# Feed-forward stages of a hybrid decoder step: 512-column weight parts, a seeded PSUM bank and a TensorE order written out

## The chip, the cores and the metric

The kernel runs on one core of one Trainium2 chip. The metric is the device time of one execution in microseconds (us); "before" is the median of three runs. All traces are of one profiled execution.

## The reference, cut to what matters

One step of a decoder layer over 1032 tokens (1024 of a prompt, 8 single decode tokens): a half-step feed-forward network, a mixer (dilated attention and a state space scan), cross attention, a second half-step feed-forward network, and a final norm. The change touches the two feed-forward networks alone:

```python
def swiglu(x, w_gate, w_up, w_down):
    return (jax.nn.silu(x @ w_gate) * (x @ w_up)) @ w_down
...
    x = x + (0.5 * swiglu(rms_norm(x, g_ffn1), w1_gate, w1_up, w1_down)).astype(x.dtype)
    ...
    x = x + (0.5 * swiglu(rms_norm(x, g_ffn2), w2_gate, w2_up, w2_down)).astype(x.dtype)
```

with x of 1032 x 1024, the two wide weights 1024 x 2816 and the third 2816 x 1024, all float32.

## The kernel before, in words

**Precision.** Each float32 factor is split in two float32r parts, hi (a rounding copy) and lo (the rest). A product takes three matmuls: hi hi, hi lo, lo hi (`three`, L341 to L345).

**Products of 2 x 2 blocks.** Tokens, which run along the columns of every matmul, fall in three groups: P0 and P1 of 388 columns, and R of 256. P0 and P1 go through a seven-product form of the 2 x 2 block product (Winograd's form of Strassen's algorithm): the weight side needs A11, A12, A21, A22 and the sums S1 = A21 + A22, S2 = S1 - A11, S3 = A11 - A21, S4 = A12 - S2; the token side B11, B21, B22 and T1 to T4. Then C11 = A11 B11 + A12 B21, C12 = U2 + S1 T1 + S4 B22, C21 = U3 + A22 T4, C22 = U3 + S1 T1, with U2 = A11 B11 + S2 T2 and U3 = U2 + S3 T3. Group R is multiplied plainly with the A blocks, in matmuls of 256 columns.

**Loops.** `ffn` walks over pairs of 128 hidden features. `gate_up(m)` runs twice per pair (22 per network): it makes gate and up products of 128 hidden features; its two weight loads of 512 KB give A11, A12 (gate) and A21, A22 (up). `down(m0)` then multiplies the pair's hidden values with two rows of blocks of the third weight and adds to x: two halves c of the output, two units u each (10 per network). The last pair is done plainly by `down_last`. A `gate_up` has 84 matmuls of 388 columns and 48 of 256, and a `down` has as many. In `gate_up` each weight block has four chunks j of 128 columns, each with its own input.

**Weights.** `weights` (L307) makes each factor in pieces of 256 columns: DVE forms a sum where one is needed (L321), ACT casts to hi (L331), DVE and POOL in turn subtract to get lo (L332). Parts live in a ring of four tiles of 1024 columns (tag "w"): one is the sums of the block, three hold two pieces with hi and lo each. Raw weights have two tiles (tag "wr"), loaded on the SP queue (L338).

**PSUM.** A `gate_up`, or a unit of `down`, has a set of four banks: b1, b2, b3 for the seven products and rb for group R; sets are taken from the pools anew and in turn. `ORDER` (L355) lists the products with bank, token factor and whether the bank starts anew. `evac` follows each: A11's product is copied to SBUF as `e["s"]` by ACT (L389, L469), and added wherever U2 or U3 is needed (by DVE in `gate_up`, L392, L398, L418; by POOL in `down`, L472, L478, L485). S1's and S4's results are read from b3 by DVE (L401, L404); S4's product is added to b3 after S1's result has been read. In `down` DVE adds each bank to x (L471 to L486).

**Who sets the order.** The program is traced, and a planner with a timing model orders each engine's instructions; TensorE's too, so products of one block and of the next, R's and the seven, lie mixed on TensorE. Each engine then runs its queue in that order, and waits on semaphores.

Of the kernel before, what the change touches and what calls it, by code (L numbers as in the profile page):

```python
# [10 lines left out]
F32 = mybir.dt.float32  # L11
# [9 lines left out]
T = SEQ + NDEC  # L21
# [31 lines left out]
def _shape_constants():  # L53
    """Arrays that depend on the shapes alone."""
# [11 lines left out]
    # decode tokens' heads on the partitions: token b's head e in row 32 (b % 4) + 8 (b // 4) + e, and in row 8 b + e  # L66
# [10 lines left out]
def tile_step(ctx, tc, a, o):  # L77
# [59 lines left out]
    def banks(shape, bufs):  # L137
        """Divides the last two banks anew."""
# [27 lines left out]
    def rstd(out, ms):  # L166
        """out = 1/sqrt(ms + eps) for a few columns: an estimate from the exponent, then Newton's steps."""
# [10 lines left out]
    def rstd_row(acc, one):  # L178
        """1/rms of up to 400 tokens on all partitions (in PSUM), from sums of squares by feature."""
# [21 lines left out]
    def nstat(N, x, k, ti, eng=nc.gpsimd):  # L201
        """Adds the squares of a finished block; after the last one the row 1/rms."""
# [10 lines left out]
    def nsplit(N, x, k, s):  # L213
        """hi/lo parts of x * gain."""
# [7 lines left out]
    def wload(src, dve=0, dst=None):  # L222
        """Loads a block of weights and splits it in two float32r parts, w = hi + lo."""
# [26 lines left out]

# [16 lines left out]
    def factors(es, side, F, names):  # L267
        """Tiles for the parts of a normalized input, block by block of its features."""
# [38 lines left out]
    def weights(raw):  # L307
        """Hi/lo parts of a weight block's factors, 256 columns at a time."""
        S = {}
        sums = wt("fs", F32)  # L310
        done = []

        def get(name, c):
            if name in raw:
                return raw[name][:, c * 256:(c + 1) * 256]
            if (name, c) not in S:
                p, q, op, i = {"S1": ("A21", "A22", OP.add, 0), "S2": ("S1", "A11", OP.subtract, 1),
                               "S3": ("A11", "A21", OP.subtract, 0), "S4": ("A12", "S2", OP.subtract, 1)}[name]
                p, q = get(p, c), get(q, c)
# [4 lines left out]
        def mat(name, c):  # L324
            src = get(name, c)
            i = len(done) % 2 * 512
            if not i:
                st["wt"] = wt("fw", F32R)
# [1418 lines left out]
```

## Time and profile before

| what | value |
|---|---|
| runs, us | 2729.35, 2729.98, 2732.21; median 2729.98 |
| profiled execution, span from first to last instruction, us | 2729.3 |
| granted TensorE clock, mean | 0.973 of full speed |
| first network's products, us of the span | about 106 to 841 |
| second network's products, us of the span | about 1948 to 2709 |

The profiled execution's span lies 0.7 us under the median, so times of the trace can be set against the runs as they are. The profile page gives busy shares by engine and in 40 slices of the span; matmuls are pipelined, so their busy share says little, and the start-to-start distance of matmuls in the timeline is what is read for TensorE's rate. A wait is shown in the timeline in brackets, with what ended it.

### The profile page before, as it was taken

What the parts mean: (1) busy time and instruction counts of PE and PEld (TensorE: products, weight loads), DVE (VectorE), ACT (ScalarE), POOL (GpSimd) and SP (SyncE); (2) the same over time, 40 slices, a digit from 0 to 9 for tenths busy, and PEclk for the clock granted to TensorE, in tenths of its full rate; (3) what the DMA queues carried; (4) which work ended last, traced back from release to release, by engine and by line L of the source; (5) the groups of instructions that cost most, each with busy time, mean ns of one, the idle gap of its engine ahead of it and who ended that gap; (6) DMA issues with size and microseconds to landing.
All of it is one profiled execution on the core that took longest, in us unless ns stands there. A gap on an engine that the chain in (4) does not pass through costs nothing. (4 is left out here: it accounts for less than half of the span.)

```text
span 2729.3 us, 44428 instructions
## 1 busy us (share of the span) xinstructions
PE 2512.2 (92%) x15995; PEld 2380.5 (87%) x15995; DVE 2118.6 (78%) x4455; ACT 1179.2 (43%) x2817; POOL 1314.5 (48%) x1246
## 2 busy tenths in 40 slices
PE   6999999999999999987987899989799999999998
PEld 5899999999998999886676799978689999999997
DVE  7677787888876668989789957564888888787886
ACT  5533333344344456554466423233443333333345
POOL 5555555555563114436365644102455555555553
PEclk8999999999999999998998999999899999999999
DMA  5411112111123222235755324573011111111112
GB/s 168 133 48 60 59 57 62 56 56 56 56 67 111 63 62 83 80 117 188 232 181 173 110 72 137 174 234 98 17 47 47 47 47 47 54 49 53 49 47 78
DMA packets 274404, 243.81 MB, mean 89 GB/s; under 512 B 17008, under 2 KB 246056, under 8 KB 274176
## 3 DMA queue, kind: packets, MB, share of 16 engines
q1 hardware_dynamic: 272512, 240.88, 28.7%
q8 instruction: 126, 2.06, 0.3%
q14 instruction: 94, 0.77, 0.1%
q10 hardware_dynamic: 1672, 0.09, 0.0%
HBM read 200.02 MB, written 45.75 MB: 90 GB/s over the span
## 5 line engine op out<-in xcount | busy, mean ns | idle before, releaser
L331 ACT CAST fw<-fs 128x256 fp32r<-128x256 f32 x512 | 192.7, 405 | 446.3 <-DVE fs L321 303.7
L332 POOL TENSOR_TENSOR fw<-fs,fw 128x256 fp32r<-128x256 f32 x256 | 216.4, 846 | 343.4 <-ACT fw L331 329.1
L235 POOL TENSOR_TENSOR wl<-wr,wh 128x1024 fp32r<-128x1024 f32 (+4 forms) x79 | 168.3, 2131 | 406.4 <-ACT wh L231 393.6
L332 POOL TENSOR_TENSOR fw<-fraw,fw 128x256 fp32r<-128x256 f32 x262 | 212.0, 815 | 108.6 <-ACT fw L331 95.4
L331 ACT CAST fw<-fraw 128x256 fp32r<-128x256 f32 x524 | 187.9, 403 | 158.0 <-PE pd L345 53.3
L332 DVE TENSOR_TENSOR fw<-fs,fw 128x256 fp32r<-128x256 f32 x256 | 159.3, 622 | 60.7 <-ACT fw L331 60.6
L321 DVE TENSOR_TENSOR fs<-fraw 128x256 f32<-128x256 f32 x256 | 166.7, 667 | 29.7 <-DMA fraw<-in_w_up_dram 26.1
L332 DVE TENSOR_TENSOR fw<-fraw,fw 128x256 fp32r<-128x256 f32 x262 | 141.6, 541 | 59.4 <-ACT fw L331 57.8
L345 PE MATMUL pd<-hRh,fw 128*128 128x256 f32 x640 | 136.6, 280 | 0.0
L231 ACT CAST wh<-wr 128x1024 fp32r<-128x1024 f32 (+1 forms) x80 | 76.6, 958 | 99.6 <-PE pwa L245 41.4
L472 POOL TENSOR_TENSOR x<-x,ts 128x388 f32<-128x388 f32 x80 | 93.3, 1175 | 45.0 <-PE pd L345 37.9
L345 PEld LDWEIGHTS pd<-hRh,fw 128*128 128x128 f32 x640 | 110.5, 189 | 0.0
L478 POOL TENSOR_TENSOR x<-x,ts 128x388 f32<-128x388 f32 x80 | 91.2, 1161 | 36.6 <-DVE x L477 36.6
L418 DVE TENSOR_TENSOR tu<-pg,ts 128x388 f32<-128x388 f32 x44 | 24.7, 562 | 107.3 <-PE pg L345 107.3
L856 DVE SCALAR_TENSOR_TENSOR tg<-xr,hv,tg 128x344 f32<-128x344 f32 (+1 forms) x108 | 84.2, 786 | 16.8 <-ACT tg L854 16.1
L485 POOL TENSOR_TENSOR x<-x,ts 128x388 f32<-128x388 f32 x80 | 89.1, 1113 | 15.8 <-DVE x L484 15.8
L245 PE MATMUL pxbc<-xh,wh 128*128 128x344 f32 x288 | 96.6, 335 | 0.0
L245 PE MATMUL pxbc<-xl,wh 128*128 128x344 f32 x288 | 95.7, 332 | 0.0
L245 PE MATMUL pxbc<-xh,wl 128*128 128x344 f32 x288 | 95.4, 331 | 0.0
L321 DVE TENSOR_TENSOR fs<-fraw,fs 128x256 f32<-128x256 f32 x128 | 93.7, 732 | 1.9 <-POOL fw L332 1.8
L245 PE MATMUL pqkv<-xh,wh 128*128 128x344 f32 x288 | 93.7, 325 | 0.5 <-ACT tg L207 0.5
L245 PE MATMUL pqkv<-xh,wl 128*128 128x344 f32 x288 | 93.2, 324 | 0.0
(801 smaller groups left out, 9773.9 us busy)
## 6 DMA issues: line engine op xcount, KB each, us to landing
fraw<-in_w_gate_dram SPq DMA_DIRECT2D x44, 512.0 KB
fraw<-in_w_up_dram SPq DMA_DIRECT2D x44, 512.0 KB
fraw<-in_w_down_dram SPq DMA_DIRECT2D x44, 512.0 KB
wr<-in_w_in_dram SPq DMA_DIRECT2D x32, 512.0 KB
x_scr<-x SPq DMA_DIRECT2D x16, 516.0 KB
x<-x_scr SPq DMA_DIRECT2D x16, 516.0 KB
bc<-acs_scr SPq DMA_DIRECT2D x16, 512.0 KB
ckv<-in_cache_mem_k_dram SPq DMA_DIRECT2D x16, 512.0 KB
```

What stands on the lines that cost most here:

```text
L231: nc.scalar.copy(hi[:, :w], raw[:, :w])
L235: e.tensor_sub(lo[:, q], raw[:, q], hi[:, q].bitcast(F32))
L245: nc.tensor.matmul(ps, w, v, start=i == 0, stop=i == last)
L321: nc.vector.tensor_tensor(t, p, q, op=op)
L331: nc.scalar.copy(hi, src)
L332: (nc.vector if len(done) % 2 else nc.gpsimd).tensor_sub(lo, src, hi.bitcast(F32))
L345: nc.tensor.matmul(ps, l[:, js], m, start=bool(start and not i), stop=bool(stop and i == 2), skip_group_check=True)
L418: nc.vector.tensor_add(u0, b2, e["s"])
L472: nc.gpsimd.tensor_add(xa[:, P1], xa[:, P1], e["s"])
L478: nc.gpsimd.tensor_add(xb[:, P1], xb[:, P1], e["s"])
L485: nc.gpsimd.tensor_add(xb[:, P0], xb[:, P0], e["s"])
L856: nc.vector.scalar_tensor_tensor(cv, raw[:, i:i + c], hw(i), cv, op0=OP.mult, op1=OP.add)
```

## The change

Only `ffn` and its helpers change (the other hunks drop comments):

- The pieces of weights are 512 columns wide: a whole block with its four chunks in `gate_up`; two blocks of 256 (A11 with A21, S1 with S2, A12 with A22, S3 with S4) in `down`. One ring tile holds hi and lo of one piece. Sums in `gate_up` are 512 wide, in `down` 256.
- The sums have a tile of their own, in the room of the row 1/rms (`held`), for all blocks but the first of a network; the four ring tiles then all hold parts. S3 is written over S1, and S4 over S2.
- A11's product is copied by ACT from b1 into b2 (PSUM to PSUM), and S2's product is added onto that. So U2 and U3 are plain ACT copies of b2 in `gate_up` (DVE adds before), C21 needs one DVE instruction less, and in `down` the three POOL adds of `e["s"]` per unit go. A matmul per set at the start of a network writes b2 once, so that later matmuls add to it.
- The eight banks are taken once per network, as two fixed sets.
- In S4's evac for odd m, T2's two steps come ahead of B22 and T3. In `down` each unit's evac follows its own matmuls.
- `tc.manual_schedule(engines={PE})` around each `gate_up` and each `down`: TensorE runs a block's instructions in the order in which the program emits them. Where they fall among those of other blocks, and the order on the other engines, stay the planner's. The emitted order of `gate_up` is A11, R by A11, S2, A12, R by A12, S3, S1, S4, A22, R by A22, R by A21; in the first block of a network all of R comes last. In `down`, for each c: A11, R by A11, R by A21, S1, S2, A12, R by A12, S3, S4, A22, R by A22.

```diff
-            hi, lo = st["wt"][:, i:i + 256], st["wt"][:, i + 256:i + 512]
-            nc.scalar.copy(hi, src)
-            (nc.vector if len(done) % 2 else nc.gpsimd).tensor_sub(lo, src, hi.bitcast(F32))
+    def two(n):
+
+        t = wt("fw", F32R)
+        return t[:, :n], t[:, n:2 * n]
+
+    def split(hl, src, like=lambda t: t):
+
+        hi, lo = like(hl[0]), like(hl[1])
+        st["turn"] = not st.get("turn")
+        nc.scalar.copy(hi, src)
+        (nc.vector if st["turn"] else nc.gpsimd).tensor_sub(lo, src, hi.bitcast(F32))
+        return hl
...
-    ORDER = (("A11", 0, "B11", True), ("S2", 1, "T2", True), ("A12", 0, "B21", False), ("S3", 1, "T3", False),
+    ORDER = (("A11", 0, "B11", True), ("S2", 1, "T2", False), ("A12", 0, "B21", False), ("S3", 1, "T3", False),
              ("S1", 2, "T1", True), ("S4", 2, "B22", False), ("A22", 1, "T4", False), ("A21", None, None, False))
...
+        def sums_of(m):
+            if not m:
+                return wt("fs", F32)
+            if not held:
+                held.append(rp.tile([128, T], F32, name="fs", tag="r"))
+            return held[0]
+
+        sets = [[PD("fb") for _ in range(3)] + [PO("fb")], [flat(PT("fb")) for _ in range(2)] + [PS("fb"), PS("fb")]]
...
+        for bk, _ in sets:
+            h = F["B11"][0][0]
+            nc.tensor.matmul(bk[1], h[:, :128], h, start=True, stop=True, skip_group_check=True)
...
+            def mat(name):
+                if name == "S2":
+                    add_up("S1", t, sums[:, :512])
+                if name in SUMS and name not in t:
+                    add_up(name, t, sums[:, :512] if name == "S3" else sums[:, 512:1024])
+                return split(two(512), t[name])
...
             def evac(name):
                 if name == "A11":
-                    e["s"] = acc_(PA)
-                    nc.scalar.copy(e["s"], b1)
+                    nc.scalar.copy(b2, b1)
                 elif name == "S2":
                     e["U2"] = acc_(PA)
-                    nc.vector.tensor_add(e["U2"], b2, e["s"])
+                    nc.scalar.copy(e["U2"], b2)
...
                 elif name == "S3":
                     e["U3"] = acc_(PA)
-                    nc.vector.tensor_add(e["U3"], b2, e["s"])
+                    nc.scalar.copy(e["U3"], b2)
                 elif name == "S1":
                     e["u1"] = sq_(PA)
                     nc.vector.tensor_add(e["u1"], b3, e["U3"])
...
                         b12, t1 = Hd["b"]
+                        nc.vector.tensor_sub(t1, u1, t1)
+                        put(Hd["T2"], t1, nc.vector)
                         put(Hd["B22"], u1, nc.gpsimd)
                         nc.vector.tensor_sub(b12, u1, b12)
-                        nc.vector.tensor_sub(t1, u1, t1)
-                        put(Hd["T2"], t1, nc.vector)
                         put(Hd["T3"], b12, nc.gpsimd)
                 elif name == "A22":
                     u0, u1 = sq_(PA), e["u1"]
-                    nc.vector.tensor_add(u0, b2, e["s"])
-                    nc.vector.scalar_tensor_tensor(u0, u0, 0.5, e["g0"], op0=OP.mult, op1=OP.mult)
+                    nc.vector.scalar_tensor_tensor(u0, b2, 0.5, e["g0"], op0=OP.mult, op1=OP.mult)
...
                 if name == "S3":
-                    early = {("S1", c): mat("S1", c) for c in range(2)}
...
+                    early["S1"] = mat("S1")
+                w = early.pop(name, None) or mat(name)
+                if f:
+                    for j in range(4):
+                        three(bk[b], w, j, F[f][j], first and j == 0, j == 3)
+                if f:
+                    evac(name)
+                if name[0] == "A" and not late:
+                    rest(name, w)
...
                     if name == "A11":
-                        e["s"] = acc_(PA)
-                        nc.scalar.copy(e["s"], b1)
+                        nc.scalar.copy(b2, b1)
                     elif name == "S2":
                         add(xa[:, P1], xa[:, P1], b2)
-                        nc.gpsimd.tensor_add(xa[:, P1], xa[:, P1], e["s"])
...
+                    need(name)
+                    w = W[name]
+                    if f:
                         for e in U:
-                            three(e["b"][b], w, e["j"], Hd[t], first, True)
+                            three(e["b"][b], w, e["j"], Hd[f], first, True)
+                            evac(name, e)
...
             for i in range(2):
-                gate_up(m + i)
+                with tc.manual_schedule(engines={mybir.EngineType.PE}):
+                    gate_up(m + i)
...
             if m < last:
-                down(m)
+                with tc.manual_schedule(engines={mybir.EngineType.PE}):
+                    down(m)
```

## Rows read from the trace of the kernel before

**Rows 1.** Profile page: busy us, share of the span and instructions of each engine.

```profile
PE 2512.2 (92%) x15995; PEld 2380.5 (87%) x15995; DVE 2118.6 (78%) x4455; ACT 1179.2 (43%) x2817; POOL 1314.5 (48%) x1246
```

**Rows 2.** Stretches: us, busy PE, PEld, DVE, ACT, POOL (count), granted clock, DMA share, GB/s.

```profile
148.83:810.65 661.82, 632.24 (x3962) 615.59 (x3961) 532.74 (x1046) 258.75 (x692) 374.47 (x402) 1.00 0.19 57
2019.12:2681.34 662.22, 632.97 (x3962) 615.68 (x3960) 536.34 (x1047) 257.00 (x691) 370.59 (x398) 1.00 0.16 49
595.50:613.00 17.50, 17.50 (x115) 17.50 (x114) 10.47 (x23) 6.73 (x18) 6.00 (x9) 1.00 0.17 61
613.00:634.00 21.00, 18.30 (x116) 17.39 (x114) 20.97 (x41) 9.55 (x26) 15.15 (x16) 1.00 0.15 42
```

**Rows 3.** Timeline (start us, us, engine, instruction) of TensorE in a `gate_up`: S1's end, R, A22, S4.

```profile
605.69 0.34 PE L345 MATMUL pg<-T13h,fw 128*128 128x388 f32 x1
605.87 0.28 PE L345 MATMUL pg<-R4h,fw 128*128 128x256 f32 x1
...
607.53 0.34 PE L345 MATMUL pg<-T40h,fw 128*128 128x388 f32 x1
...
609.64 0.34 PE L345 MATMUL pg<-B220h,fw 128*128 128x388 f32 x1
...
611.80 0.28 PE L345 MATMUL pg<-R0h,fw 128*128 128x256 f32 x1
```

**Rows 4.** TensorE's waits in ten pairs of the first network: us, times, longest.

```profile
PE pd L345 <- ACT T2h L264: 18.7, 10, 2.7
PE pd L345 <- DVE fw L332: 8.5, 10, 0.9
```

**Rows 5.** Timeline at a `down`'s first wait: ACT and TensorE.

```profile
618.06 0.51 ACT L264 CAST T2h<-tu 128x388 fp32r<-128x388 f32 x1 [1.31 <-DVE tu L413]
...
618.64 0.42 PE L345 MATMUL pd<-B22h,fw 128*128 128x388 f32 x1 [1.76 <-ACT T2h L264]
```

**Rows 6.** Timeline of DVE about S1's and S4's results in a `gate_up`.

```profile
606.07 0.56 DVE L401 TENSOR_TENSOR tu<-pg,ts 128x388 f32<-128x388 f32 x1 [0.52 <-PE pg L345]
...
609.84 0.56 DVE L418 TENSOR_TENSOR tu<-pg,ts 128x388 f32<-128x388 f32 x1 [2.88 <-PE pg L345]
```

**Rows 7.** Timeline of the second network's first block, TensorE.

```profile
1951.02 0.43 PE L345 MATMUL pg<-B210h,fw 128*128 128x388 f32 x1
...
1964.99 0.69 PE L345 MATMUL pg<-T20h,fw 128*128 128x388 f32 x1 [11.60 <-ACT T20h L264]
...
1980.69 0.53 PE L345 MATMUL pg<-T23h,fw 128*128 128x388 f32 x1
1983.31 0.69 PE L345 MATMUL pg<-T30h,fw 128*128 128x388 f32 x1 [2.10 <-DVE ts L392]
```

**Rows 8.** Groups by line and shape: count, busy us, mean ns, idle before.

```profile
L480 DVE TENSOR_TENSOR x<-x,pd 128x388 f32<-128x388 f32 x80 | 43.7, 546 | 0.0
L321 DVE TENSOR_TENSOR fs<-fraw,fs 128x256 f32<-128x256 f32 x128 | 93.7, 732 | 1.9 <-POOL fw L332 1.8
L321 DVE TENSOR_TENSOR fs<-fs,fraw 128x256 f32<-128x256 f32 x128 | 52.0, 435 | 0.0
L472 POOL TENSOR_TENSOR x<-x,ts 128x388 f32<-128x388 f32 x80 | 93.3, 1175 | 45.0 <-PE pd L345 37.9 <-DVE x L471 7.1
```

**Rows 9.** As rows 8, for 512 columns and for ACT's copies.

```profile
L231 ACT CAST wh<-wr 128x512 fp32r<-128x512 f32 x16 | 9.8, 614 | 31.7 <-PE pwa L245 21.0 <-PE pco L245 6.3 <-issue 4.3
L389 ACT COPY ts<-pg 128x388 f32<-128x388 f32 x44 | 21.1, 479 | 1.6 <-PE pg L345 1.6
...
L1547 DVE TENSOR_TENSOR ql<-q,qh x16: 668/684/2516, 1685.3 to 1849.5; 128x512 fp32r<-128x512 f32 x16
...
L265 POOL TENSOR_TENSOR lwl<-fraw,lwh 128x512 fp32r<-128x512 f32 x8 | 10.6, 1348 | 10.1 <-ACT lwh L264 10.1
```

**Rows 10.** A load's issue on the SP queue, and DVE's instruction that waits for it.

```profile
586.61 0.37 SPq L338 DMA_DIRECT2D fraw<-in_w_up_dram  x1
...
590.41 0.76 DVE L321 TENSOR_TENSOR fs<-fraw 128x256 f32<-128x256 f32 x2 [0.58 <-DMA fraw<-in_w_up_dram]
```

More of the change, by code (lines that the diff above doesn't have):

```diff
@@ L305, in prep_r @@
             put(F["R"][k], b, nc.gpsimd if k % 2 else nc.vector)
[L307 to L319, printed above, removed]
-                S[name, c] = t = sums[:, (i * 2 + c) * 256:(i * 2 + c + 1) * 256]
-                nc.vector.tensor_tensor(t, p, q, op=op)
-            return S[name, c]
[L324 to L328, printed above, removed]
-            done.append(name)
-            hi, lo = st["wt"][:, i:i + 256], st["wt"][:, i + 256:i + 512]
-            nc.scalar.copy(hi, src)
-            (nc.vector if len(done) % 2 else nc.gpsimd).tensor_sub(lo, src, hi.bitcast(F32))
-            return hi, lo
-        return mat
+    SUMS = {"S1": ("A21", "A22", OP.add), "S2": ("S1", "A11", OP.subtract), "S3": ("A11", "A21", OP.subtract),
+            "S4": ("A12", "S2", OP.subtract)}
+    def two(n):
[7 more added lines that the diff above has]
+        return hl
     def raw_(src):
@@ L365, in gate_up @@
-            a21, a22 = raw_(cols_of(wu, m * 128))
-            mat = weights({"A11": a11, "A12": a12, "A21": a21, "A22": a22})
-            b1, b2, b3, rb = bank_set("pg")
-            b1, b2, b3 = (b[:, :PA] for b in (b1, b2, b3))
-            rb = rb[:, :2 * NR].rearrange("p (i t) -> p i t", t=NR)
-            bk = (b1, b2, b3)
-            e = {}
-            def rest(name, w, c):
+            g_, u_ = raw_(cols_of(wg, m * 128)), raw_(cols_of(wu, m * 128))
+            t = {"A11": g_[:, :512], "A12": g_[:, 512:], "A21": u_[:, :512], "A22": u_[:, 512:]}
@@ L374, in rest @@
+            bk, rb = bank_set()
+            b1, b2, b3 = bk
+            sums = sums_of(m)
+            e = {}
+            def mat(name):
[4 more added lines that the diff above has]
+                return split(two(512), t[name])
+            def rest(name, w):
                 i = name in ("A21", "A22")
                 first, last = name in ("A11", "A22"), name in ("A12", "A21")
-                for j in range(2):
-                    k = c * 2 + j + (4 if name in ("A12", "A22") else 0)
-                    three(rb[:, int(i)], w, j, F["R"][k], first and c + j == 0, last and c + j == 2)
+                for j in range(4):
+                    three(rb[:, int(i)], w, j, F["R"][j + (4 if name in ("A12", "A22") else 0)], first and j == 0, last and j == 3)
@@ L433, in gate_up @@
             early = {}
-            for name, b, t, first in ORDER:
+            for name, b, f, first in ORDER:
                 if late and name == "A21":
@@ L437, in gate_up @@
                 if name == "S3":
-                    early = {("S1", c): mat("S1", c) for c in range(2)}
-                for c in range(2):
-                    w = early.pop((name, c), None) or mat(name, c)
-                    if t:
-                        for j in range(2):
-                            three(bk[b], w, j, F[t][c * 2 + j], first and c + j == 0, c + j == 2)
-                    if name[0] == "A" and not late:
-                        rest(name, w, c)
-                evac(name)
+                    early["S1"] = mat("S1")
@@ L447, in gate_up @@
+                w = early.pop(name, None) or mat(name)
+                if f:
+                    for j in range(4):
+                        three(bk[b], w, j, F[f][j], first and j == 0, j == 3)
[3 more added lines that the diff above has]
+                    rest(name, w)
             if late:
                 for name in ("A11", "A12", "A22", "A21"):
[L449 to L450 removed]
+                    rest(name, mat(name))
@@ L451, in gate_up, with pair, need @@
             rest_end()
         def down(m0):
-            wa, wb = (raw_(wd[m * 128:(m + 1) * 128]) for m in (m0, m0 + 1))
-            mat = weights({"A11": wa[0], "A21": wa[1], "A12": wb[0], "A22": wb[1]})
+            ra, rb_ = (raw_(wd[m * 128:(m + 1) * 128]) for m in (m0, m0 + 1))
+            sums = sums_of(1)
+            twice = lambda t: t.rearrange("p (i c) -> p i c", i=2)
             for c in range(2):
+                cs = slice(c * 256, (c + 1) * 256)
+                wa, wb = twice(ra)[:, :, cs], twice(rb_)[:, :, cs]
+                t = {"A11": wa[:, 0], "A21": wa[:, 1], "A12": wb[:, 0], "A22": wb[:, 1]}
+                W = {}
+                def pair(names, src):
+                    hi, lo = split(two(512), src, twice if len(src.shape) == 3 else (lambda x: x))
+                    for i, name in enumerate(names):
+                        W[name] = hi[:, i * 256:(i + 1) * 256], lo[:, i * 256:(i + 1) * 256]
+                def need(name):
+                    if name in W:
+                        return
+                    if name in ("A11", "A21"):
+                        pair(("A11", "A21"), wa)
+                    elif name in ("A12", "A22"):
+                        pair(("A12", "A22"), wb)
+                    else:
+                        i = 0 if name in ("S1", "S2") else 2
+                        for j, nm in enumerate((("S1", "S2"), ("S3", "S4"))[i // 2]):
+                            add_up(nm, t, sums[:, (i + j) * 256:(i + j + 1) * 256])
+                        pair(("S1", "S2") if i == 0 else ("S3", "S4"), sums[:, i * 256:(i + 2) * 256])
```

46 lines of the change are left out of this document (24 added, 22 removed).

## The prediction

> **What bounds the kernel now.** I read the page's busy lines first. TensorE is busy 92%, DVE 78%, no other engine half of the span [rows 1]. A busy TensorE need not run at its rate, so I next took the distance between matmul starts in the timeline. In a `gate_up` 12 matmuls of 388 columns lie between 607.53 and 609.64 and 12 between 609.64 and 611.80: 0.176 to 0.180 us each, taken as 0.177. Fourteen of 256 columns lie between 605.87 and 607.53: 0.119 each [rows 3]. The granted clock is 1.00 there, the upper level of 2.4 GHz [rows 2], so this rate is the floor.
>
> Then the stretches. From the first product of the first `down` to the first of `down_last` each network does ten pairs, one `down` and two `gate_up`s each: 252 matmuls of 388 columns and 144 of 256, so 252 x 0.177 + 144 x 0.119 = 61.74 us per pair at the floor. The stretches took 661.82 and 662.22 us [rows 2], 66.2 per pair. So 1324.0 - 20 x 61.74 = 89.2 us in all, 4.46 per pair, are all that TensorE loses in them, and this is the most that the change can gain there.
>
> Where are they lost? TensorE's waits name `down`: per pair 1.87 us for T2h of ACT and 0.85 for a lo part of DVE [rows 4]. The rest is a matmul's overlap lost at each wait, and smaller waits. DVE is busy 20.97 of 21.00 us in the stretch of a `down`, but 10.47 of 17.50 in that of a `gate_up` [rows 2]: `down` is bound by DVE, `gate_up` by TensorE alone, whose products run there without a gap.
>
> **The change part by part.** My sum is
>
> time = 2729.3 - 89.2 + 44 s + 20 d + e
>
> with s the new loss per `gate_up` (22 per network), d what is left of the loss per `down`, and e the two starts and ends of the networks.
>
> *s: S4 right behind S1.* This is the price of the written order. S4's product is added to b3, and DVE must have read S1's result from b3 first. Today the planner puts R's products and A22's between: S1 ends at 605.69 + 0.34, S4 starts at 609.64, and DVE has read b3 long before [rows 3, 6]. In the emitted order nothing stands between, and whatever is queued behind S4 on TensorE waits with it. The price: from the start of S1's last matmul 0.34 to its end, 0.04 until DVE starts (606.03 to 606.07), 0.56 for DVE [rows 6], 0.07 until TensorE starts, as between ACT's end at 618.57 and the matmul at 618.64 [rows 5]. That is 1.01 us in place of 0.18: 0.83 lost if DVE is free. The other bound is the one such handshake that stands open today, between S2 and S3 at a network's start: 2.10 us behind a busy DVE [rows 7]. In a `gate_up` DVE is idle over a third of the time, 2.88 us before S4's result for one [rows 6], and A21's lo part, the one due then, falls to POOL in the turn of two. I take 0.9, near the lower end. The rest of the block can't fill the gap, its order being fixed; the next block's A11 can't, as its ring tile comes free only when S1's product has ended. 44 x 0.9 = 39.6 us.
>
> *The other handshakes of `gate_up`* are covered. S2 waits for ACT's copy of b1 to b2, which R's twelve products (1.43 us) hide: 0.34 + 0.04 + 0.48 [rows 9] + 0.07 - 0.18 = 0.75. No row shows ACT writing to PSUM; between the 0.48 of a copy to SBUF and the 0.61 of ACT's cast of 512 columns [rows 9] the cover holds, and without it (the first block, where R comes last) it costs 0.75 to 0.9 once per network. U2's copy is hidden by A12 and R (3.5 us), U3's by S1 (2.1 us).
>
> *d: `down`.* Three things go. T2 is started two DVE steps earlier, and in the new order S4 stands before A22 and two R's, so from S4's end to T2's use lie 2.1 + 2.9 us of the `gate_up` and 1.1 + 1.4 + 1.1 us of the `down`, 8.6 us. The chain is two DVE steps and a SiLU on ACT before u1, then one DVE step, ACT's cast and DVE's lo, about 0.55 each, 3.3 us with today's durations. So the 1.87 goes, and A12's factor B21 is next, also early. POOL's adds to x go, 12 per `down` of 1.15 us, three groups like the one of [rows 8]: 13.8 of POOL's some 15 us. And per `gate_up` DVE loses two adds and half of another step. What is left on DVE per `down` are 24 adds to x of 0.546 [rows 8], back to back every 0.47 and so 11.3, eight smaller ones (2.7), eight sums of 0.44 to 0.73 [rows 8], four lo parts of 512 columns at 0.68 [rows 9], and some 3 us of the hidden values: 23 to 26 us against 20.6 of products (61.74 / 3), and the `gate_up`s around it take 2 to 4 of them. So DVE is about level with TensorE. S3's adds are the tightest: 0.9 us of slack before A22's product. d lies between 0.2 and today's 4.5; I take 1.0, the size of one DVE instruction that stands in the way, near the lower end, as two of the waits lose their cause. 20 x 1.0 = 20.
>
> The trace has DVE's sums of raw tiles at 0.73 on average where POOL is busy, against 0.44 for those of finished sums [rows 8]. The Trainium skill (SBUF — State Buffer, Who interferes with whom) says that a DVE instruction with two SBUF inputs contends with a GpSimd one that reads SBUF; by it, with POOL's adds gone, nearly all of that excess would go, d would be 0.2 and the sum 16 us lower.
>
> *Weights.* ACT's cast of 512 columns is 0.61, DVE's lo 0.68, POOL's 1.35 [rows 9]. They hide behind TensorE if a part is ready in time. Tightest is S2 of the next block: the up weights' tile is free when A21 is split, about 14 us into a block of 21.4; the load lands 3.8 us later [rows 10]; two sums, cast and POOL's lo take 0.7 + 0.7 + 0.6 + 1.4, so S2 is ready at 21.2, due at 24.9. 3.7 us of cover; the SP queue has the same loads in the same order. If the cover goes, each us over it costs one us per block.
>
> *e.* In the second network's first block TensorE waits 11.60 us for T2 and does A12's product (B21) before that wait, and S1's (T1) between T2's [rows 7]. In the written order both come behind T2: 24 x 0.177 = 4.2 us more, at half the clock (0.32 each, as between 1980.69 and its neighbours) up to 7.7. I take 5, 1 for the first network's start, 1 for the ends. The four dummy matmuls cost 0.2 each at most: nothing. e = 7, from 4 to 10.
>
> Sum: 2729.3 - 89.2 + 39.6 + 20 + 7 = 2706.7 in the profiled execution's span; the runs' median lies 0.7 above it: 2707.
>
> **The rivals.**
>
> *1, slower: the open handshake meets a busy DVE.* S1's result waits behind a 512-wide DVE instruction. For it: pieces are twice as long, 0.68 instead of some 0.41, more beside POOL, and DVE's order is the planner's. Against: DVE is idle 40% of a `gate_up`, and lo parts come in turns. If each meets one and a half, s = 1.9: 2729.3 - 89.2 + 83.6 + 20 + 7 = 2751. It decides from s = 1.4 with d = 1 (no gain). The Trainium skill (Perfetto Trace Analysis, Optimizing Scalar/DVE Operations) has this rule against wide pieces: where an engine isn't saturated but causes bubbles on others, smaller instructions may let work finish sooner. DVE isn't saturated in `gate_up` [rows 2], so it bears there.
>
> *2, no change: `down` stays bound by DVE.* 23 to 26 us of DVE work against 20.6, as above. With d = 2.1 the sum is 2729. For it: DVE's 20.97 of 21.00 [rows 2]. Against: with POOL quiet and two lo parts' fixed costs gone, the work shrinks from some 28 us.
>
> *3, faster: the order isn't what is emitted.* The planner may still lay blocks into each other; if something fills the gap behind S1, s = 0 and the time is 2667. Against: no ring tile is free for it.
>
> *4, slower: a part of the weights comes late*, 1.5 us per block: 66 us more, 2773. Against: 3.7 us of cover.
>
> **How the numbers follow.** Chances: the forecast (2680 to 2722) 0.53, rival 3 0.07, rival 2 (2722 to 2735) 0.15, rival 1 0.18, rival 4 and the like 0.07. A measurement of this kernel can tell about 0.2%, 5.5 us, from no change. Faster: 0.53 + 0.07 = 0.60; the same, rival 2 but for its edge, 0.14; slower: 0.18 + 0.07 and the edge 0.01, 0.26. The range: below, s = 0.83, d = 0.2 and e = 4 give 2685, and 2680 leaves out rival 3; above, s = 1.4, d = 2.5 and e = 10 give 2762, which leaves out the worst of rivals 1 and 4.
>
> **What would show it.** In the trace after: between S1's last product and S4's first on TensorE a wait of 0.6 to 0.7 us that DVE's add from b3 ends, 44 times, right for s; no wait for T2h; a pair every 64.5 us, of which `down` 21 to 22; DVE under 95% in `down`; x adds on DVE alone. Wrong would be: waits for `fw` parts in `gate_up` (rival 4), a wait behind S1 over 1.2 us (rival 1), a `down` of 23 us or more with DVE full (rival 2), or other products between S1 and S4 (rival 3).

## The result, and the profile after

The changed kernel is slower: 2831.33 us median (2827.53 to 2833.79) against 2731.10 before, a ratio of 1.0367 (95% interval 1.0352 to 1.0383). The forecast was 2707, the range ended at 2762. The profiled execution has a span of 2828.0 us, 98.7 more than before.

Busy time by engine, from the profile page of after; against [rows 1] DVE fell by 182 us and POOL by 310, and the kernel got slower all the same:

```profile
PE 2544.3 (90%) x15999; PEld 2404.5 (85%) x15999; DVE 1936.9 (68%) x3888; ACT 1165.1 (41%) x2387; POOL 1004.2 (36%) x747
```

The same stretches as in [rows 2], from the first product of the first `down` to the first of `down_last`, with the unchanged stages between the networks, and one `down` (columns: us, busy PE, PEld, DVE, ACT, POOL with counts, granted clock, DMA share, GB/s):

```profile
153.64:845.60 691.96, 642.26 (x3962) 622.20 (x3961) 442.23 (x784) 249.45 (x492) 222.61 (x160) 1.00 0.17 53
845.60:1990.90 1145.30, 1045.21 (x6789) 960.75 (x6788) 854.22 (x1975) 521.69 (x1125) 439.34 (x325) 0.96 0.42 128
2066.75:2784.00 717.25, 649.84 (x3962) 630.31 (x3960) 450.72 (x787) 251.23 (x490) 211.22 (x158) 0.98 0.14 45
429.40:458.20 28.80, 25.47 (x147) 24.26 (x145) 24.75 (x47) 9.08 (x20) 11.32 (x8) 0.94 0.18 58
```

The stages between the networks in the kernel before:

```profile
810.65:1947.80 1137.15, 1040.49 (x6788) 959.16 (x6787) 851.09 (x1980) 523.15 (x1130) 435.91 (x323) 0.96 0.42 129
```

The ten pairs take 691.96 and 717.25 us where they took 661.82 and 662.22: 30.1 and 55.0 more. With the floor of 61.74 per pair, the loss per pair is now 7.5 and 10.0 us, from 4.4 and 4.5. The stages between, whose code didn't change, take 1145.3 in place of 1137.2 (8.1 more), the networks' starts 4.8 and 4.5 more (153.64 against 148.83; 2066.75 - 1990.9 = 75.9 against 2019.12 - 1947.8 = 71.3), and the end 4.0 less. Before rounding these add up to the 98.7. The loss is in the pairs, where the gain was forecast.

What TensorE waits for there, first network, then second (us in total, times, longest); [rows 4] is the same of before:

```profile
PE fb L332 <- DVE x L501: 20.1, 20, 2.0
PE fb L332 <- ACT fw L319: 20.0, 26, 0.8
PE fb L332 <- DVE hRl L265: 4.9, 10, 0.5
PE fb L332 <- DVE x L518: 2.9, 10, 0.3
```


```profile
PE fb L332 <- DVE tv L394: 33.2, 10, 3.8
PE fb L332 <- DVE tu L411: 14.5, 20, 0.7
PE fb L332 <- DVE x L501: 7.6, 14, 0.9
PE fb L332 <- ACT fb L399: 6.9, 9, 1.0
```

The waits for T2h and for a lo part of [rows 4] are gone, as forecast. Four kinds have come in their place. One is the handshake from S1 to S4 (`tu L411`; in the first network 19 of the 26 waits put down to `ACT fw L319` are it, as that ACT cast ends 0.06 us later than DVE's add; the other seven stand before A22's product in `down`, where DVE's add of S3's sum, L505, ends at about the same time as the cast). One is the rest group: its bank, which DVE must have read before `down` uses it again (`tv L394`), and the lo part of its hidden value (`hRl`). One is S2's sum, which DVE must add to x before S3's product may go onto the same bank (`x L501`). The fourth, in the second network alone, is ACT's copy of the seed in a `gate_up` (`fb L399`): on ACT it stands behind a cast of the rest group's value, which comes late from DVE. Here is the first, in the timeline of the second network:

```profile
2058.47 0.34 PE L332 MATMUL fb<-T13h,fw 128*128 128x388 f32 x1
...
2058.92 0.56 DVE L411 TENSOR_TENSOR tu<-fb,ts 128x388 f32<-128x388 f32 x1 [2.96 <-PE fb L332]
...
2059.53 0.44 PE L332 MATMUL fb<-B220h,fw 128*128 128x388 f32 x1 [0.72 <-DVE tu L411]
```

From S1's last matmul to S4's first lie 1.06 us, 0.18 of which is the matmul's own step. The second kind is the costliest. DVE, POOL, ACT and TensorE at a `down`'s start, second network:

```profile
2066.69 1.02 POOL L265 TENSOR_TENSOR B22l<-tu,B22h 128x388 fp32r<-128x388 f32 x1 [0.77 <-ACT B22h L264]
2066.74 1.39 DVE L265 TENSOR_TENSOR T2l<-tu,T2h 128x388 fp32r<-128x388 f32 x1
...
2067.66 1.32 POOL L265 TENSOR_TENSOR T3l<-tu,T3h 128x388 fp32r<-128x388 f32 x1
...
2068.05 1.22 DVE L366 TENSOR_TENSOR fs<-fraw 128x256 f32<-128x256 f32 x1
2068.05 0.28 PE L332 MATMUL fb<-hRh,fw 128*128 128x256 f32 x1
...
2068.95 1.44 POOL L320 TENSOR_TENSOR fw<-fs,fw 128x512 fp32r<-128x512 f32 x1
2069.19 1.75 DVE L320 TENSOR_TENSOR fw<-fraw,fw 128x512 fp32r<-128x512 f32 x1
2070.86 0.41 DVE L366 TENSOR_TENSOR fs<-fs,fraw 128x256 f32<-128x256 f32 x1
2071.20 0.41 DVE L394 SCALAR_TENSOR_TENSOR tv<-fb,tv 128x256 f32<-128x256 f32 x1
...
2071.64 0.41 ACT L264 CAST hRh<-tv 128x256 fp32r<-128x256 f32 x1 [2.62 <-DVE tv L394]
...
2071.66 0.38 PE L332 MATMUL fb<-hRh,fw 128*128 128x256 f32 x1 [3.33 <-DVE tv L394]
```

TensorE stands for 3.3 us at the fourth matmul of R by A11. That is the first one of the second unit, and in the kernel its bank is the one in which the last `gate_up` left its rest group: DVE must read it first (`tv`, L394), which it starts at 2071.20. No value is missing: in the kernel R by A11 takes the hidden value of the pair's first `gate_up` in both units, and that of the second, which R by A12 needs, is cast only from 2071.64 to 2072.05, when TensorE already goes on. ACT's SiLU, the other input of L394, had ended by 2067.34. DVE was not idle; three instructions of 388, 256 and 512 columns ahead of it took 1.39, 1.22 and 1.75 us while POOL worked beside it, where the same forms take 0.55, 0.42 and 0.69 alone. That L394 stands behind them on DVE is the planner's order; another order on DVE wasn't tried.

### The profile page after: what moved, and what is told of

It reads as the page before. It is cut to its first block, busy times and chain, and to the rows that moved or that the text cites. A ratio compares the mean times of both kernels' runs of the same rounds, so it can differ in the third digit from the quotient of the medians.

```text
span 2828.0 us, 42475 instructions
## 1 busy us (share of the span) xinstructions
PE 2544.3 (90%) x15999; PEld 2404.5 (85%) x15999; DVE 1936.9 (68%) x3888; ACT 1165.1 (41%) x2387; POOL 1004.2 (36%) x747
## 5 line engine op out<-in xcount | busy, mean ns | idle before, releaser
L320 POOL TENSOR_TENSOR fw<-fraw,fw 128x512 fp32r<-128x512 f32 x131 | 189.9, 1450 | 493.0 <-ACT fw L319 492.9
L320 POOL TENSOR_TENSOR fw<-fs,fw 128x512 fp32r<-128x512 f32 x128 | 177.0, 1383 | 455.6 <-ACT fw L319 402.7
L319 ACT CAST fw<-fraw 128x512 fp32r<-128x512 f32 x262 | 162.4, 620 | 277.7 <-PE fb L332 250.0
L319 ACT CAST fw<-fs 128x512 fp32r<-128x512 f32 x256 | 158.3, 619 | 199.1 <-DVE fs L366 131.9
L366 DVE TENSOR_TENSOR fs<-fraw 128x512 f32<-128x512 f32 (+1 forms) x168 | 116.9, 696 | 167.8 <-DMA fraw<-in_w_up_dram 88.5
L320 DVE TENSOR_TENSOR fw<-fraw,fw 128x512 fp32r<-128x512 f32 x131 | 100.1, 764 | 163.5 <-ACT fw L319 161.6
L332 PE MATMUL fb<-hRh,fw 128*128 128x256 f32 x640 | 138.9, 288 | 33.7 <-DVE tv L394 33.2
L320 DVE TENSOR_TENSOR fw<-fs,fw 128x512 fp32r<-128x512 f32 x128 | 91.8, 717 | 80.5 <-ACT fw L319 79.7
L332 PEld LDWEIGHTS fb<-hRh,fw 128*128 128x128 f32 x640 | 109.6, 192 | 38.8 <-DVE tv L394 35.2
L245 PE MATMUL pqkv<-xl,wh 128*128 128x344 f32 x288 | 92.8, 322 | 0.0
L332 PE MATMUL fb<-T3h,fw 128*128 128x388 f32 x160 | 52.5, 369 | 27.7 <-DVE x L501 27.7
```

Source lines behind the costliest of these rows:

```text
L245: nc.tensor.matmul(ps, w, v, start=i == 0, stop=i == last)
L319: nc.scalar.copy(hi, src)
L320: (nc.vector if st["turn"] else nc.gpsimd).tensor_sub(lo, src, hi.bitcast(F32))
L332: nc.tensor.matmul(ps, l[:, js], m, start=bool(start and not i), stop=bool(stop and i == 2), skip_group_check=True)
L366: nc.vector.tensor_tensor(dst, t[p], t[q], op=op)
```

## The experiments

Each kernel is built from the one after, unless the text says otherwise. "Pairs" is the time of the two stretches of ten pairs, first and second network; "between" that of the unchanged stages.

| kernel | median, us | pairs, us | between, us |
|---|---|---|---|
| before | 2731 | 661.8, 662.2 | 1137 |
| after | 2831 | 692.0, 717.3 | 1145 |
| e1_free_down | 2778 | 670.6, 688.9 | 1141 |
| e2_free_all | 2704 | 645.8, 641.5 | 1147 |
| e3_r_between | 2810 | 684.4, 693.2 | 1156 |
| e4_turn | 2795 | 695.7, 683.5 | 1145 |
| e5_r_before_s4 | 2807 | 686.3, 693.4 | 1151 |
| e6_down_r_late | 2749 | 672.7, 659.0 | 1150 |
| e7_before_fixed | 2828 | 707.6, 706.0 | 1151 |
| e8_free_turn | 2708 | 640.1, 636.8 | 1155 |
| e9_pool_quiet | 2765 | 669.2, 670.7 | 1148 |
| e10_free_unseeded | 2724 | 644.4, 649.6 | 1158 |
| e11_free_e6order | 2723 | 648.5, 650.4 | 1153 |
| e12_half_e6order | 2736 | 659.1, 657.6 | 1150 |
| e13_free_quiet | 2686 | 630.2, 619.9 | 1162 |
| e14_free_dve_lo | 2695 | 635.7, 635.8 | 1150 |

The last column matters: the planner places the whole program anew for each kernel, and code that no kernel touches takes 1137 to 1162 us. A difference of 10 us in the median can come from there; where that is so the pairs are read instead.

### Is it the written order?

Two theories were set against each other. Theory 1: the written order, since in it one late result stops all of TensorE. Theory 2: DVE's load at the start of `down`, which comes late in any order.

**e1_free_down** and **e2_free_all** take the order away: e1 by the second of these edits, e2 by both.

```diff
             for i in range(2):
-                with tc.manual_schedule(engines={mybir.EngineType.PE}):
-                    gate_up(m + i)
+                gate_up(m + i)
...
-                with tc.manual_schedule(engines={mybir.EngineType.PE}):
-                    down(m)
+                down(m)
```

> The changed kernel with TensorE's order left to the planner in down alone; gate_up keeps its written order. In the changed kernel the pair stretches lose 7.5 us per pair in the first network and 10.0 in the second, of which 1.9 are the two S1 to S4 handshakes, so 5.6 and 8.1 are lost in each down. Theory 1 (the written order: every late result of DVE stops all of TensorE, since nothing may be pulled ahead): the loss per down falls to 2.5 or less, about 2831 - 20 x 4.4 = 2745. Theory 2 (DVE's load: hidden values, sums and lo parts are piled at the start of down, its two-input instructions are lengthened beside POOL, and this comes late in any order): the loss stays within a fifth, 2805 to 2835.

> The changed kernel without any written order, in gate_up and in down. Theory 1 (order): S1 to S4's 0.93 us per gate_up go too, some 41 us, and down's loss as in the kernel that frees down alone: about 2705. Theory 2 (load): only the handshake goes, 2790. If the planner gives the same order unasked, 2831.

Measured: 2778 and 2704. With `down` alone free, the loss per pair falls by 2.1 and 2.8 us, 50 us in all: between the theories. With both free it falls to 2.8 and 2.4 us, and the kernel is 1.0% faster than before (ratio 0.9898, 0.988 to 0.9916). So the rest of the change is a gain, and the written order costs 128 us on top of it. The free kernel's pairs:

```profile
152.70:798.60 645.90, 628.71 (x3963) 620.79 (x3961) 408.20 (x786) 248.76 (x490) 199.88 (x159) 0.99 0.18 57
2017.10:2658.50 641.40, 633.11 (x3961) 614.84 (x3959) 416.59 (x787) 248.99 (x490) 204.53 (x158) 1.00 0.16 50
```

In the free kernel S1's last product starts at 379.99 in one `gate_up` and S4's first at 386.37; between them the planner put S3's products, R and part of A22's:

```profile
379.99 0.34 PE L332 MATMUL fb<-T13h,fw 128*128 128x388 f32 x1
380.17 0.34 PE L332 MATMUL fb<-T30h,fw 128*128 128x388 f32 x1
...
382.29 0.28 PE L332 MATMUL fb<-R4h,fw 128*128 128x256 f32 x1
...
385.13 0.34 PE L332 MATMUL fb<-T40h,fw 128*128 128x388 f32 x1
...
386.37 0.34 PE L332 MATMUL fb<-B220h,fw 128*128 128x388 f32 x1
```

**e7_before_fixed** is the kernel before with the two `manual_schedule` regions as its only edit.

> The kernel before with one part of the change alone: TensorE's order in gate_up and down is that in which the program emits it. Pieces, sums, POOL's adds and buffers are those of before. Theory 1 (the written order is what costs): the handshake from S1 to S4 costs 0.8 to 0.9 us per gate_up here too, 40 us, and down's losses grow from 4.5 to 6 or more per pair: 2732 + 40 + 30 to 100, so 2800 to 2870. Theory 2 (DVE's load at the start of down, brought by the wide pieces and the sums): the handshake alone, 2772 or less.

Measured: 2828, 96 us slower than before (ratio 1.0353, 1.0337 to 1.0368), with a loss of 9.0 and 8.9 us per pair. Neither wide pieces nor seeds nor sums are in it, so a written order by itself can cost as much as the whole change. That the two losses are alike is chance: the order written out is the one that the kernel before emits, and it ran into other waits, on x adds (`x L486`, `x L477`) above all. The 40 us expected for S1 to S4 didn't come: in all but 4 of 44 `gate_up`s the planner placed the next block's A11 between. The pairs, and the largest waits of the first network:

```profile
145.00:852.70 707.70, 645.64 (x4009) 623.02 (x4010) 537.98 (x1056) 263.07 (x696) 364.50 (x401) 1.00 0.17 53
2073.60:2779.60 706.00, 644.32 (x4008) 621.17 (x4009) 542.09 (x1058) 261.35 (x695) 359.17 (x399) 1.00 0.15 46
```

```profile
PE pg L345 <- DVE x L486: 14.9, 10, 1.5
PE pd L345 <- DVE x L477: 12.0, 12, 1.2
PE pd L345 <- DVE x L486: 11.1, 10, 1.1
PE pd L345 <- DVE tv L383: 9.0, 10, 2.0
```

### Which places of the order?

**e3_r_between** moves R by A12 behind S1.

```diff
...
-                if name[0] == "A" and not late:
+                if name[0] == "A" and name != "A12" and not late:
                     rest(name, w)
+                if name == "S1" and not late:
+                    rest("A12", wa12)
```

> The changed kernel with one move in the written order of gate_up: R's products with A12 stand behind S1's product instead of before S3's, so 1.43 us of products lie between S1 and S4. If the 0.93 us per gate_up before S4 are the bare latency of TensorE to DVE to TensorE (0.04 + 0.56 + 0.07 with 0.34 of the last matmul), all of it goes: 2831 - 44 x 0.93 = 2790, and down is as before. If they are DVE being busy with something else, the wait goes along behind R's products and the time stays over 2815.

Measured: 2810. The wait before S4 is gone in both networks, bar the first block of each, where the move doesn't apply; so it was the bare latency. But 21 us came of the 41 (the pairs gained 32, the stages between lost 11), and in the first network the wait for the lo part of the rest group's value grew from 4.9 to 13.0 us:

```profile
PE fb L332 <- DVE x L504: 13.1, 20, 0.9
PE fb L332 <- DVE hRl L265: 13.0, 10, 1.3
```

**e5_r_before_s4** writes `gate_up` as A11, R, S2, A12, R, S3, S1, R by A22, R by A21, S4, A22.

```diff
-            for name, b, f, first in ORDER:
...
+            for step in ("A11 rA11 S2 A12 S3 S1 S4 A22" if late else "A11 rA11 S2 A12 rA12 S3 S1 rA22 rA21 S4 A22").split():
```

> The changed kernel, all of it in a written order, with another order in gate_up: S1, then R's products with A22 and A21 (2.86 us), then S4, A22. It covers the handshake from S1 to S4, and R's last product stands 4.3 us ahead of the end of gate_up instead of at its end, so the rest group's hidden value is ready when down asks for it right after its first product. Theory 1 (in a written order what matters is which result each product waits for, and what stands between): S1 to S4 goes (20 us per network) and the wait for the hidden value (5 in the first, 33 in the second network): 2831 - 78 = 2753. Theory 2 (DVE's load at the start of down sets the pace): the waits go along to the next product that needs DVE, 2795 or more.

Measured: 2807, which is theory 2's side. Both waits that it aimed at are gone (that for `tv` was one for the bank, as shown above, not for the value). But A22, now last, feeds B21 of `down`, and that is now late:

```profile
PE fb L332 <- DVE B21l L265: 31.5, 10, 3.8
PE fb L332 <- DVE x L503: 8.5, 10, 1.0
```

**e6_down_r_late** adds the same kind of move to `down`: R by A11 and by A21 stand behind S2.

```diff
-                for name, b, f, first in (ORDER[i] for i in (0, 7, 4, 1, 2, 3, 5, 6)):
+                for step in "A11 S1 S2 rA11 rA21 A12 rA12 S3 S4 A22 rA22".split():
...
```

> As the kernel with R before S4, and in down R's products with A11 and A21 stand behind S2 instead of before S1. So 1.43 us more of products lie between S2 and S3, which waits until DVE has read S2's result, and the rest group's hidden value is due 2.1 us later; S1's and S2's weights are due 1.43 us earlier. Theory 1: the wait before S3 (23 us in the first, 10 in the second network) falls by two thirds or more, some 20 us below the kernel with R before S4: 2733. Theory 2: no gain, within 6 us of the kernel with R before S4, or slower where the weights come late.

Measured: 2749, 58 us below e5 where 20 were expected. 1.4 us more of products ahead of what DVE brings late take the wait for B21's lo part from 31.5 to 5.5 us in the second network:

```profile
PE fb L332 <- DVE B21l L265: 5.5, 10, 0.6
```

I read this as a half for each theory: DVE's results come late at the start of each `down`, by 2 to 4 us in most of these kernels, the product that asks first waits, and in a written order all of TensorE waits with it.

### What makes DVE late?

**e4_turn** begins the turn of DVE and POOL for lo parts alike in both networks.

```diff
         held = []
+        st["turn"] = False
```

> The changed kernel with one bit set: the turn that hands lo parts to DVE and POOL by turns begins in the second network as in the first. The first network has an odd number of lo parts (11 in its first block), so in the second DVE gets the lo parts of raw weights and POOL those of the sums, the other way round than in the first. Theory 2 (load): this is what makes the second network lose 8.1 us per down where the first loses 5.6; the 33 us of waits behind the rest group's hidden value go and the time falls by 20 to 30, to 2801 to 2811. Theory 1 (order alone): who does which lo part moves nothing beyond 6 us, 2825 to 2837.

Measured: 2795, all of it in the second network (717.3 to 683.5); the wait for `tv` is gone there. The first block of a network makes 11 lo parts, an odd number, and so in the second network POOL had the lo parts of sums and DVE those of raw weights, the other way round.

**e8_free_turn** has the same edit in the free kernel.

> The changed kernel with TensorE's order left to the planner throughout and, in addition, the turn of DVE and POOL for lo parts begun alike in both networks. In the written order this was worth 36 us (2831 to 2795). Theory 1 (a late DVE result costs only where TensorE may do nothing else meanwhile): within 8 us of the free kernel with the turn as it was, 2696 to 2712. Theory 2 (the load itself costs): it gains here too, 2685 or less.

Measured: 2708, no change. The second network's pairs gain 4.7 us, no more than the first's (5.7), where the edit changes nothing. What cost 34 us in a written order costs about nothing in a free one.

**e9_pool_quiet** takes POOL out of the blocks, all but one instruction of a pair (T1's lo part). The lo parts that POOL made are left out of the computation: ACT writes a copy of the source in their place. T3 and T4 are edited like B22.

```diff
-        (nc.vector if st["turn"] else nc.gpsimd).tensor_sub(lo, src, hi.bitcast(F32))
+        if st["turn"]:
+            nc.vector.tensor_sub(lo, src, hi.bitcast(F32))
+        else:
+            nc.scalar.copy(lo, src)
...
-                        put(Hd["B22"], u1, nc.gpsimd)
+                        put_act(Hd["B22"], u1)
```

> The changed kernel, its written order as it is, with POOL taken out of the feed-forward blocks: the lo parts that POOL makes (of weights, and of the hidden values B22, T3 and T4) are replaced by a copy of the source on ACT into the same place. So these lo parts are left out of the computation; the number of products, their order and all waits stay. DVE's own work is unchanged. In the trace of the changed kernel DVE's 512-column sums take 0.69 us alone and 1.08 beside a POOL instruction, its 256-column sums 0.42 and 0.98, some 100 us of excess in both networks; in one down four of them in a row take 5.1 us in place of 2.1. Theory 2 (load, and what POOL adds to it): DVE is 2 to 3 us less late at the start of down, and the time falls by 20 x 2.5 = 50, to 2780 or below. Theory 1 (order alone): DVE's lateness is set by the chain of its instructions and stays; no more than 15 us are gained, 2816 or more.

Measured: 2765, 66 us less, in the written order as it was. DVE's own instructions are the same ones; two groups of after, then of e9, first network (count, busy us, mean ns, idle before):

```profile
L366 DVE TENSOR_TENSOR fs<-fraw,fs 128x256 f32<-128x256 f32 x19 | 18.9, 993 | 0.3
...
L265 DVE TENSOR_TENSOR B21l<-tu,B21h 128x388 fp32r<-128x388 f32 x11 | 15.0, 1364 | 1.6 <-ACT B21h L264 1.6
```


```profile
L373 DVE TENSOR_TENSOR fs<-fraw,fs 128x256 f32<-128x256 f32 x19 | 8.0, 423 | 0.3
...
L265 DVE TENSOR_TENSOR B21l<-tu,B21h 128x388 fp32r<-128x388 f32 x11 | 6.8, 622 | 17.9 <-ACT B21h L264 17.9
```

993 ns became 423, and 1364 became 622. A part of the 66 us may be that ACT's copy (0.62 us) is ready sooner than POOL's lo part (1.35); the run doesn't divide the two.

**e13_free_quiet** is e9 with a free order, the fourth corner; it leaves out the same lo parts.

> The kernel with the quiet POOL (its lo parts, of weights and of the hidden values B22, T3 and T4, are replaced by a copy of the source on ACT and so are left out of the computation), with TensorE's order left to the planner. Corners so far: written order 2831, written and quiet 2765, free 2704. If DVE's lateness costs only where the order is written, quieting gains little here: 2690 or more. If the two add up: 2704 - 66 = 2638, or, since the free kernel loses 2.6 us per pair in all, at the least 2660 or less.

Measured: 2686, between what the two sides allowed. In the pairs, quieting POOL brings 69 us in the written order (1409.2 to 1340.0) and 37 in the free one (1287.3 to 1250.1); the stages between hide 15 of the latter in the median. So the two neither add up nor are the same thing: the free order hides about half of what POOL costs. Without POOL and free, TensorE is at its floor, with 1.3 and 0.3 us lost per pair.

**e14_free_dve_lo** takes all lo parts of weights in `gate_up` to DVE, in the free order.

```diff
-        (nc.vector if st["turn"] else nc.gpsimd).tensor_sub(lo, src, hi.bitcast(F32))
+        (nc.vector if dve or st["turn"] else nc.gpsimd).tensor_sub(lo, src, hi.bitcast(F32))
...
-                return split(two(512), t[name])
+                return split(two(512), t[name], dve=m > 0)
```

> The changed kernel with a free order, and in gate_up all lo parts of weights on DVE (four more of 0.69 us per gate_up, where DVE is busy half of the time), those of down by turns as they were. Nothing is left out. If what is left of the loss in the free kernel (2.8 and 2.4 us per pair) comes from lo parts of POOL that lengthen DVE's work or arrive late: 2685 to 2695. If gate_up is bound by TensorE alone and down by DVE's own work: 2704, within 8 us.

Measured: 2695 (2693.4 to 2696.0), at the edge of what either theory allowed. The pairs gain 16 us, with DVE busier and POOL at 96.5 us in place of 199.9 in the first network. It beats the kernel before and the one after: 0.9870 of the time before (0.9854 to 0.9887).

### Which part of the rest brings the gain?

**e10_free_unseeded** undoes the seeding in `down`, with POOL's twelve adds back, in the free order.

```diff
                     if name == "A11":
-                        nc.scalar.copy(b2, b1)
+                        e["s"] = acc_(PA)
+                        nc.scalar.copy(e["s"], b1)
                     elif name == "S2":
                         add(xa[:, P1], xa[:, P1], b2)
+                        nc.gpsimd.tensor_add(xa[:, P1], xa[:, P1], e["s"])
...
```

> The changed kernel with a free order (2704), and one part of the change undone: in down the shared first product isn't seeded in PSUM; ACT copies it to SBUF, and POOL adds it to x, 12 adds of 1.15 us per down, as before the change. If the seeding is what the free order gains on the kernel before (28 us), as the prediction reckoned it: 2704 + 28 = 2732, with DVE's adds lengthened beside POOL. If the wide pieces bring the gain: within 8 us of 2704.

Measured: 2724, between the two. The pairs lose 1.4 less and 8.1 more, 6.7 us in all; the other 14 come from the unchanged stages and the second network's start. So the seeding in `down` brings about a fifth of the 36.7 us that the free kernel's pairs gain on before, as far as two placements by the planner can tell; that in `gate_up` stays in this kernel. Which other part brings the rest (wide pieces, sums in their own buffer, T2 first) wasn't tried.

**e11_free_e6order** and **e12_half_e6order** give e6's sequence to the planner, in both parts or in `down` alone.

> The kernel with R before S4 and with R late in down, with no written order: the planner gets the work in this sequence and places it as it finds it ready. If the sequence of emission matters to the planner as it does in a written order (2831 to 2749), it gains here too: 2690 or less. If the planner makes its own order of it: 2704, within 8 us.

> As the kernel with R before S4 and R late in down (2749), with gate_up in its written order and down left to the planner. In that gate_up no product waits for a result that stands right before it, so a written order should cost nothing there. Theory 1: the loss per pair falls from 5.5 and 4.2 us to that of the wholly free kernel, 2.8 and 2.4: 2749 - 45 = 2704. Theory 2: the load in down keeps half of it, 2725 or more.

Measured: 2723 and 2736. Neither side had allowed for 2723: a sequence that was better written out is no better as a suggestion, and in e11 TensorE now waits 40 us for T2's lo part. In e12 the loss per pair is 4.2 and 4.0, where e6 had 5.5 and 4.2, with a `gate_up` whose own handshakes are covered: theory 2's side, though by no one wait; the largest in the first network is that for the seed's copy on ACT, 9.1 us.

## Why the prediction was wrong

**The floor and the loss of before** held: 61.74 us per pair is the floor, and e13 comes within 0.3 us of it.

**s** held. Forecast 0.9, measured 0.9 (1.06 - 0.18), by the very terms of the sum, with DVE free. Rival 1 did not come: bar once, at a start, DVE was free when S1 ended. No run here shows the Trainium skill's rule on smaller instructions (Perfetto Trace Analysis, Optimizing Scalar/DVE Operations) to help: the 256-column pieces of e7 lost 9.0 us per pair in a written order, after's wide ones 8.7 in the mean, but e7 differs in more than the width.

**d** is the step that failed: forecast 1.0 per `down`, measured (174.4 - 40 x 0.9) / 20 = 6.9, with 174.4 = 691.96 + 717.25 - 20 x 61.74. This lumps all of the loss that isn't S1 to S4. It lies outside the bounds given, 0.2 to 4.5. Three faults lie in it.

First, `gate_up`'s written order was walked product by product for results that stand right before their use; `down`'s only for T2 and for S3's adds. For the rest d was taken from sums of work, DVE's against TensorE's. The walk would have found the rest group: R by A21 ends the `gate_up`, and 1.4 us into the `down` R by A11 goes onto the same bank, with ACT's SiLU and a DVE step to read it before. That cost 33.2 us. It would have found S3's product as well, which waits until DVE has added S2's sum to x (27.7 us in both networks); the text named only S3's own adds, before A22's product, as the tightest.

Second, today's 4.5 was taken as the upper bound. It is the loss of a free order, in which TensorE does something else meanwhile; a written order has no such bound. e7 shows it by itself.

Third, DVE was judged by its total. The total was right: 23 to 26 us were forecast, and it is busy for 24.75 of 28.8 us in the `down` shown above. But the work bunches. The two halves of that `down`:

```profile
429.38:443.60 14.22, 12.69 (x69) 11.88 (x68) 13.96 (x25) 5.10 (x12) 7.96 (x6) 0.88 0.12 37
443.60:458.20 14.60, 12.79 (x81) 12.40 (x79) 10.80 (x24) 4.00 (x8) 3.39 (x3) 1.00 0.24 78
```

In the first half, where hidden values, sums and lo parts meet, DVE is busy 98% of the time, in the second 74%. So rival 2's full DVE did come, for half of each `down`.

**The sentence on POOL** drew a wrong conclusion from a right rule. The Trainium skill (SBUF — State Buffer, Who interferes with whom) says that a DVE instruction with two SBUF inputs contends with a GpSimd one that reads SBUF, and the traces agree: 993 ns beside POOL, 423 without. But with its x adds gone POOL wasn't quiet. Its lo parts remain, and those of the hidden values fall right on the start of `down`. Summed over the pairs of both networks, what DVE's additions and subtractions took beyond their durations alone fell by about half, from 224 to 121 us, where the forecast by that rule had nearly all of it go; and what is left falls where TensorE waits. In `down` the sums of this group took 0.99 on average in the first network and 0.59 in the second ([rows 8], 0.73, mixes `down` and `gate_up`).

**Rival 3** was dismissed with "no ring tile is free for it". The tiles are not the point: the free planner fills the gap behind S1 with S3, R and A22 of the same block (e2). Its 2704 for the free kernel is close to the forecast of 2707, but that is no credit to the sum: there s is 0 and the loss per pair 2.6.

**Weights** held: no wait of TensorE for a raw load or POOL's part over 0.5 us in the pairs. **T2** held. **e** was 7, measured 10, from other terms: 8.1 of it are the unchanged stages, which were in no term. The starts cost 4.8 and 4.5 where 1 and 5 were taken, 1.8 of which in each is s of the first two `gate_up`s; most of the rest in the first is the seed, not covered where R comes last, at 2.8 us in place of 0.75: ACT makes it behind two casts, one of which waits for S2's sum:

```profile
108.95 0.62 ACT L319 CAST fw<-fs 128x512 fp32r<-128x512 f32 x1 [2.85 <-DVE fs L366]
109.48 0.61 ACT L319 CAST fw<-fraw 128x512 fp32r<-128x512 f32 x1
110.00 0.47 ACT L399 COPY fb<-fb 128x388 f32<-128x388 f32 x1
```
```profile
110.52 0.53 PE L332 MATMUL fb<-T20h,fw 128*128 128x388 f32 x1 [2.81 <-ACT fb L399]
```

The ends took 4.0 less, where 1 more was taken. With what was measured the sum is 2729.3 - 89.2 + 44 x 0.9 + 20 x 6.9 + 10 = 2828, as it must be, since d and e were read from the same trace.

## What to carry to other kernels

Before an engine's order is written out, walk it: for every instruction, note which result of another engine it needs and which bank another engine must have read, what stands between, and how late that engine may be at that point; a free order can do something else meanwhile, so its losses are no bound for a written one. An engine that is half idle on average can still be late by some microseconds where its work bunches, and an engine beside it that shares its reads makes that worse. Test the order by itself first: here one edit (e7) showed what a written order can cost, and one (e2) the gain that it hid.

## What the runs showed of the hardware

A DVE subtraction or addition of two SBUF operands took 0.42, 0.55 and 0.69 us at 256, 388 and 512 columns alone, and up to 1.22, 1.39 and 1.75 in the one window shown above, beside POOL: twice to three times as long, in a kernel where POOL had less to do than before. DVE's adds to x, which have one operand in PSUM, weren't lengthened: 0.55 on average at 388 columns before, beside a busy POOL ([rows 8]), and in e9 without it.

A second loss goes with TensorE's longer waits: with waits of up to 3.8 us the mean granted clock in the second network's pairs fell from 1.00 [rows 2] to 0.98. Between 2.4 and 1.2 GHz, 2% of clock means that 4% of the time ran at 1.2 GHz, which costs up to 14 of the 717 us. In e7, which lost 9 us per pair in waits of at most 2.0 us, it stayed at 1.00, and in e9, with waits of at most 1.4 us there, it is back at 1.00:

```profile
2047.80:2718.50 670.70, 630.84 (x3962) 616.60 (x3960) 392.25 (x784) 320.36 (x640) 9.26 (x9) 1.00 0.15 48
```
